# Making the operands of block products kind by kind over the direct tiles, their remainders by adding transfers, and rounding the direct tiles among the block products

## The chip, the core and the metric

The kernel runs on one core of one Trainium2 chip. The core has a matrix engine (TensorE; PE in the profile, with its weight loads as PEld), three elementwise engines (VectorE or DVE, ScalarE or ACT, GpSimd or POOL) and SyncE (SP), whose queue issues most of the loads. Transfers are issued from the queues of SP, ACT or POOL and carried out by 16 DMA engines; a transfer from POOL's queue can add to what stands at its destination. The metric is the time of one execution in microseconds (us); lower is better.

## What is computed

One decoder layer on 512 tokens of width 1024, in float32: two SwiGLU feed-forward halves (inner width 2816) around a hybrid mixer, each behind an RMSNorm, then a last RMSNorm. The change is in the first part of the two feed-forward halves.

```python
def rmsnorm(x, g):
    x32 = x.astype(jnp.float32)
    y = x32 * lax.rsqrt(jnp.mean(x32 * x32, axis=-1, keepdims=True) + EPS)
    return (y * g.astype(jnp.float32)).astype(x.dtype)

def swiglu(x, w_gate, w_up, w_down):
    return (jax.nn.silu(x @ w_gate) * (x @ w_up)) @ w_down
...
x = x + 0.5 * swiglu(rmsnorm(x, ffn1_norm[l]), ffn1_wg[l], ffn1_wu[l], ffn1_wd[l])
x = x + hybrid_mixer(rmsnorm(x, mix_norm[l]), ...)
x = x + 0.5 * swiglu(rmsnorm(x, ffn2_norm[l]), ffn2_wg[l], ffn2_wu[l], ffn2_wd[l])
```

## The kernel before

**Layout.** Features lie on the 128 partitions, the 512 tokens in the columns. The width of 1024 is 8 blocks of 128 (`KD`), the inner width 22 (`KF`). `slot` gives one of 60 buffers of 128x512 floats; a buffer goes back to the pool when the last instruction that touches its tile has run.

**Precision.** Products run in a rounded format, float32r, and each operand is two rounded parts: a rounded copy by ScalarE (`wh` of weights, `yh`, `hh` of activations) and the remainder by VectorE (`wl`, `yl`, `hl`). A product of two operands is three matmuls: high by high, high by low, low by high (`mm3`). `split` (line 260) and `wsplit` (line 238) make such a pair; weights come through `wtiles` with three buffers each for the raw load, the high and the low part.

**A feed-forward half** has an up part (`ffn_up`, line 346) and a down part (`ffn_down`, line 507). In the up part each of 22 inner blocks needs a gate product and an up product over the 8 input blocks.

- *Direct tiles.* The first six blocks of the first half, and the first four of the second, are computed directly: 24 matmuls of 512 columns for the gate, 24 for up. Four of them run in `ffn_up`, before the rest; the first of these four carries the norm's statistics (`norm_steps`), which give `rstd`, the factor of each token. `ffn_act` (line 316) scales both results by `rstd`, applies Silu, multiplies, and splits the result into `hh` and `hl`.
- *Block products.* The other 16 (18 in the second half) are taken in pairs of inner blocks by a scheme of Strassen's kind (`strassen`, line 376): the input is cut into 2 x 2 blocks (four upper input blocks a, four lower b; the token halves `lo` and `hi`), the weights as well, and seven products of half size replace eight. Each of them is 12 matmuls of 256 columns (4 input blocks, 3 matmuls each). Gate and up of a pair follow each other as w = 0, 1, 2, ...; the seven products of one w are interleaved with those of the next. The stream begins, as (product, w): (1,0) (2,0) (6,0) (5,0) (7,0) (1,1) (2,1) (4,0) (6,1) (3,0).
- *Moving operands.* The products use seven kinds of combined input, four columns (j = 0 to 3) of each: `n11` = -a_lo (product 1), `b21` = b_lo (2), `t2` = b_hi - a_hi + a_lo (6), `t1` = a_hi - a_lo (5), `r` = a_hi - b_hi (7), `q` = b_lo - t2 (4), `n22` = -b_hi (3). Each is a tile `cm` of 128x512: the rounded copy in its first 256 columns, the remainder in the last 256. `combine` (line 326) makes all seven kinds of one j after each of the four direct tiles: two scaled copies of x, four subtractions, seven copies by ScalarE and seven remainders by VectorE.
- *Block weights.* `load` (line 392) fetches the raw weights for a w and makes two sums by transfers: SP's queue loads `s1` and `s3`, POOL's queue adds a second load to each (shown as `s`; such an issue is line 161). `prepare` (line 416) runs four products ahead (`LEAD`); for product 6 it adds `s2` = s1 + x on VectorE, and rounds. `results` (line 450) takes finished products out of the accumulators: after product 1 a copy by ScalarE (`tg`), after product 2 a subtraction, and so on; product 6 adds to the accumulator of product 1, so it follows that copy.
- *Rounding of inner blocks.* Results of block products stay float32 (`h`). `halve` (line 500) splits them: four at the end of the stream, the others at the beginning of `ffn_down`.

**What sets the order.** The stream of block products is written out by hand (`manual_schedule`): engines run it in program order. The direct tiles and `combine` before it are ordered when the program is built, by a list scheduler that places instructions on each engine by priority and by its own estimates; each engine then runs its list strictly in order. Every recorded operation has line 173 and every transfer line 161, a helper's; the names of the tiles tell them apart.

Of the kernel before, what the change touches and what calls it, by code (L numbers as in the profile page):

```python
# [9 lines left out]
F32 = mybir.dt.float32  # L10
F32R = mybir.dt.float32r
AF = mybir.ActivationFunctionType
ALU = mybir.AluOpType

P = 128
S = 512
D = 1024
KD = D // P
# [26 lines left out]
HS = S // 2  # L45
LEAD = 4
# [132 lines left out]
def hybrid_kernel(ctx, tc, xt, vec, w1u, w1d, wm, wki, wrg, watt, wrnn, wout, w2u, w2d, out):  # L179
    nc = tc.nc  # L180
    plan = Plan()
    V, A = plan.engine("DVE", nc.vector), plan.engine("ACT", nc.scalar)
    G, T = plan.engine("POOL", nc.gpsimd), plan.engine("PE", nc.tensor)
# [13 lines left out]
    f = lambda ap: ap.bitcast(F32)  # L197
    cnt = [0]
    moving = {}

    def nm(s):
        cnt[0] += 1
        return f"{s}_{cnt[0]}"

    def slot(dt=F32, name="s"):
        return plan.take("slot", big.tile([P, S], dt, tag="slot", name=nm(name)))

    def work(name="t", cols=S):
        return plan.take("tmp", tmp.tile([P, cols], F32, tag="tmp", name=nm(name)))

    def awork(name="a"):
        return patt.tile([P, S], F32, tag="att", name=nm(name))

    def psum(tag="mm"):
        return psp.tile([P, S], F32, tag=tag, name=nm(tag))
# [5 lines left out]
    x = [resid.tile([P, S], F32, name=f"x{k}") for k in range(KD)]  # L221
# [4 lines left out]
    rstd = resid.tile([P, S], F32, name="rstd")  # L226

    def col(base, k):
        return vt[:, base + k:base + k + 1]
# [12 lines left out]
    def wload(src, cols):  # L242
        r, h, l = wtiles(cols)
        Q.dma_start(r, src)
        wsplit(r, h, l)
        return h, l
# [8 lines left out]
    def gemm(ps, w, ys, ks, first=True, last=True, m=P, since=0, upto=None):  # L255
        n = len(ks)
        for i, k in list(enumerate(ks))[since:upto]:
            mm3(ps, w, slice(i * m, (i + 1) * m), ys[k], first and i == 0, last and i == n - 1)

    def split(src, h, l):  # L260
        A.activation(h, src, AF.Copy)
        V.tensor_sub(l, src, f(h))
# [27 lines left out]
    def norm_steps(*sums, blocks=range(NQ)):  # L290
        pc, n = psaux(), len(blocks)
        for i, a in enumerate(sums):
            if i:
                yield waits("PE", a)
            for j, b in enumerate(blocks):

                T.matmul(pc[:, j * QB:(j + 1) * QB], a[:, b * QB:(b + 1) * QB], mean, start=i + j == 0,
                         stop=i == len(sums) - 1 and j == n - 1)
        yield waits("ACT", pc)
        sd = small.tile([P, NQ], F32, tag="st", name=nm("sd"))[:, :n]  # L300
        A.activation(sd, pc.rearrange("p (b c) -> p b c", c=QB)[:, :n, 0], AF.Sqrt, bias=epst)
        yield waits("DVE", sd)
        rs = small.tile([P, NQ], F32, tag="m8", name=nm("rs"))[:, :n]
        V.reciprocal(rs, sd)
        yield waits("PE", rs)
        pb = psaux()[:, :n * QB]
        for j in range(n):
            T.transpose(pb[:, j * QB:(j + 1) * QB], rs[:, j:j + 1].to_broadcast([P, P]), ident)
        yield waits("ACT", pb)
        A.activation(rstd[:, blocks[0] * QB:(blocks[-1] + 1) * QB], pb, AF.Copy)  # L310

    def norm_rest(steps):
        for _ in steps:
            pass

    def ffn_act(pg, pu):
        tg, tu = work("tg"), work("tu")
        V.tensor_mul(tg, pg, rstd)
        A.activation(tg, tg, AF.Silu)
        V.tensor_mul(tu, pu, rstd)  # L320
        V.tensor_mul(tu, tu, tg)
        hh, hl = slot(F32R, "hh"), slot(F32R, "hl")
        split(tu, hh, hl)
        return hh, hl

    def combine(g, j, held):

        lo, hi = slice(0, HS), slice(HS, S)
        a, b, t, q = (slot(F32, n) for n in ("ca", "cb", "ct", "cq"))
        for o, k in ((a, j), (b, j + KD // 2)):  # L330
            V.scalar_tensor_tensor(o, x[k], col(g, k), rstd, op0=ALU.mult, op1=ALU.mult)
        V.tensor_sub(t[:, lo], a[:, hi], a[:, lo])
        V.tensor_sub(t[:, hi], b[:, hi], t[:, lo])
        V.tensor_sub(q[:, lo], b[:, lo], t[:, hi])
        V.tensor_sub(q[:, hi], a[:, hi], b[:, hi])
        for n, src, sign in (("n11", a[:, lo], -1.0), ("b21", b[:, lo], 1.0), ("t2", t[:, hi], 1.0), ("t1", t[:, lo], 1.0),
                             ("r", q[:, hi], 1.0), ("q", q[:, lo], 1.0), ("n22", b[:, hi], -1.0)):
            o = held.pop(0) if len(held) else slot(F32R, "cm")
            if sign > 0:
                split(src, o[:, lo], o[:, hi])  # L340
            else:
                A.activation(o[:, lo], src, AF.Copy, scale=-1.0)
                V.scalar_tensor_tensor(o[:, hi], src, -1.0, f(o[:, lo]), op0=ALU.mult, op1=ALU.subtract)
            moving[n].append(o)

    def ffn_up(y, wu, n0, hs, g, waiting=(), given=()):
        def weights(n, j):
            return given.pop(0) if len(given) else wload(wu[n, j], KD * P)

        moving.update((n, []) for n in ("n11", "b21", "t2", "t1", "r", "q", "n22"))  # L350
        held = []
        for n in range(n0, n0 + 4):
            tag = ("aux", "mm")[n % 2]
            pg, pu = psum(tag), psum(tag)
            gemm(pg, weights(n, 0), y, range(KD))
            w = weights(n, 1)
            if n == n0:
                norm = norm_steps(acc)
                for _ in range(3):
                    next(norm)  # L360
                gemm(pu, w, y, range(KD), last=False, upto=KD // 2)
                norm_rest(norm)
                gemm(pu, w, y, range(KD), first=False, since=KD // 2)
                hs.extend(ffn_act(*p) for p in waiting)
            else:
                gemm(pu, w, y, range(KD))
            hs.append(ffn_act(pg, pu))
            if n == n0:

                for k in ("pth", "ptl"):  # L370
                    t = ptp.tile([P, NQ * S], F32R, tag=k, name=nm("cm"))
                    held.extend(t[:, i * S:(i + 1) * S] for i in range(NQ))
            combine(g, n - n0, held)
        strassen(wu, n0 + 4, hs)

    def strassen(wu, f0, hs):
# [4 lines left out]

        lo, hi = slice(0, HS), slice(HS, S)
        H = KD // 2 * P
        count = KF - f0
        ws, pairs = [], {}
# [4 lines left out]
        def load(w):  # L392

            o = W()
            n, o.j = f0 + w // 2 * 2, w % 2
            o.first = n
            o.x = raw.tile([P, WMAX], F32, tag="raw", name=nm("wr"))
            o.s1, o.s3, o.a22 = (slot(F32, t) for t in ("s1", "s3", "a22"))
            u, v = wu[n, o.j], wu[n + 1, o.j]
            Q.dma_start(o.x, u)  # L400
            Q.dma_start(o.s1, v[:, :H])
            Q.dma_start(o.s3, v[:, :H])
            Q.dma_start(o.a22, v[:, H:])
            G.dma_start(o.s1, v[:, H:], accum_op=ALU.add)
            G.dma_start(o.s3, u[:, :H], accum_op=ALU.add)
            ws.append(o)

        stream = []
# [73 lines left out]
        with tc.manual_schedule(engines=ENGINES):  # L482
            for w in range(2):
                load(w)
            for i in range(LEAD):
                prepare(i)
            for i in range(len(stream)):
                products(i)
                if i:
                    results(i - 1)  # L490
                if i + LEAD < len(stream):
                    prepare(i + LEAD)
                else:
                    n = f0 + i + LEAD - len(stream)
                    halve(hs, n)
                if i % 7 == 3 and len(ws) < count:
                    load(len(ws))
            results(len(stream) - 1)

    def halve(hs, n):  # L500

        if type(hs[n]) is not tuple:
            hh, hl = slot(F32R, "hh"), slot(F32R, "hl")
            split(hs[n], hh, hl)
            hs[n] = hh, hl
# [71 lines left out]
    hs = []  # L577

    class Given:
# [6 lines left out]
        def pop(self, _):  # L586
            return given(self.rs.pop(0))

    ffn_up(y, w1u, 2, hs, V_G1, ((WP[0], WP[1]), (WP[2], pu)), Given(AH[1:]))


# [326 lines left out]
    for k in ("pth", "ptl"):  # L918
        q = ptp.tile([P, NQ * S], F32R, tag=k, name=nm("QI"))
# [319 lines left out]

    hs = []  # L1240
    ffn_up(y2, w2u, 0, hs, V_G2)

    def done(n):
# [11 lines left out]
    n, e = KD - 1, x[KD - 1]  # L1255
# [5 lines left out]
    a, b = CHUNKS[-1]  # L1261
# [33 lines left out]
    o = {}  # L1295
# [75 lines left out]
```

## Time and profile before

| | us |
|---|---|
| median of three runs (lowest, highest) | 1112.08 (1110.92, 1112.80) |
| the profiled execution | 1113.65 |
| its span, first to last instruction | 1111.5 |
| TensorE busy | 1084.1 (98%) |
| VectorE, ScalarE, POOL busy | 773.7, 586.2, 68.7 |
| mean granted clock of TensorE | 0.991 |

A row of the timeline has start, duration, engine, line, operation, out<-in with the names of tiles, and in brackets the idle time of the engine ahead of it with what ended it. Matmuls are pipelined, so their durations overlap, and the distance of two starts is the time that one costs. `PE`, `DVE`, `ACT` and `POOL` are the engines; `SPq` and `POOLq` are their queues. In a row of windows, busy time and count stand for PE, PEld, DVE, ACT and POOL in turn, then the granted clock, the DMA engines' mean share and GB/s. In a row on transfers, "to landing" is the time from an issue to its data standing at the destination.

### The profile page before, as it was taken

To read this page: it belongs to the slowest core of one execution; us is meant where nothing else is said; L and a number is where in the kernel's file an instruction comes from. 1 tells how busy PE (TensorE), PEld (TensorE's weight loads), DVE (VectorE), ACT (ScalarE), POOL (GpSimd) and SP (SyncE) were. 2 spreads that over 40 slices of the span, in tenths; PEclk is the share of its full clock that TensorE was granted. 3 is DMA by queue.
4 is the path that set the end of the run, shared out by engine and by line. 5 is a ranking of instruction groups with operands and counts; after the bars stand their busy time and mean duration, and the time that the engine had idled before them with its cause. 6 is when DMAs were issued, how large, how long until landed. Compare 5 with 4: busy or idle time off the path is not lost.

```text
span 1111.5 us, 16307 instructions
## 1 busy us (share of the span) xinstructions
PE 1084.1 (98%) x6184; PEld 952.2 (86%) x6184; DVE 773.7 (70%) x1412; ACT 586.2 (53%) x1057; POOL 68.7 (6%) x85
## 2 busy tenths in 40 slices
PE   9989999999999989999999999999799999999996
PEld 7869999998888767888888888888699999988885
DVE  6697777786333678998799868557877777783324
ACT  6545555564223458968785664345455555562211
POOL 0011111100000000000000000000011111100001
PEclk9999999999999999999999999999999999999999
DMA  7174777743333352233232213334467777443322
GB/s 267 39 198 116 193 163 185 191 121 87 104 94 92 106 161 63 83 99 98 77 96 79 78 34 99 111 113 139 98 180 163 185 185 196 107 126 104 99 71 75
DMA packets 55949, 135.48 MB, mean 122 GB/s; under 512 B 6592, under 2 KB 11328, under 8 KB 55872
## 3 DMA queue, kind: packets, MB, share of 16 engines
q1 hardware_dynamic: 45936, 116.58, 33.5%
q0 software_dynamic: 9792, 17.83, 10.5%
q8 instruction: 48, 0.79, 0.3%
q14 instruction: 29, 0.24, 0.1%
q10 hardware_dynamic: 144, 0.05, 0.0%
HBM read 130.24 MB, written 2.10 MB: 119 GB/s over the span
## 4 chain that ended last, share of the span: by engine, by line
PE 89%; DVE 6%; ACT 3%; DMA 1%; issue 1%; SPq 0%; DVEq 0%; ACTq 0%
PE mm L173 59%; PE aux L173 30%; DVE wl L173 1%; ACT wh L173 1%; DMA gr<-wrg 1%; DVE yl L173 1%; DVE xc L173 0%; ACT L173 0%; DVE yf L173 0%; DMA x<-xt 0%; DVE o L173 0%; ACT rl L173 0%; DVE tu L173 0%; ACT r L173 0%; DVE th L173 0%
## 5 line engine op out<-in xcount | busy, mean ns | idle before, releaser
L173 DVE TENSOR_TENSOR wl<-wr,wh 128x1024 fp32r<-128x1024 f32 (+3 forms) x204 | 193.0, 954 | 117.2 <-ACT wh L173 113.2
L173 ACT ACTIVATE wh<-wr 128x1024 fp32r<-128x1024 f32 (+4 forms) x206 | 171.2, 836 | 190.5 <-PE mm L173 69.8
L173 PE MATMUL mm<-cm,wh 128*128 128x256 f32 x1088 | 201.5, 285 | 12.0 <-ACT cm L173 6.0
L173 PEld LDWEIGHTS mm<-cm,wh 128*128 128x128 f32 x1088 | 170.9, 193 | 13.7 <-ACT cm L173 6.4
L173 PE MATMUL mm<-yh,wh 128*128 128x512 f32 (+1 forms) x416 | 164.5, 396 | 1.2 <-ACT yh L173 0.7
L173 PE MATMUL mm<-yl,wh 128*128 128x512 f32 (+1 forms) x416 | 162.8, 392 | 0.9 <-DVE yl L173 0.8
L173 PE MATMUL mm<-yh,wl 128*128 128x512 f32 x408 | 159.4, 391 | 0.0
L173 PE MATMUL mm<-cm,wl 128*128 128x256 f32 x544 | 154.7, 284 | 0.0
L173 PE MATMUL aux<-cm,wh 128*128 128x256 f32 x816 | 152.7, 286 | 0.0
L173 ACT ACTIVATE wh<-s 128x512 fp32r<-128x512 f32 x136 | 81.7, 626 | 105.3 <-DVE s L173 72.0
L173 DVE TENSOR_TENSOR wl<-s,wh 128x512 fp32r<-128x512 f32 x136 | 93.5, 690 | 54.0 <-ACT wh L173 50.8
L173 PEld LDWEIGHTS aux<-cm,wh 128*128 128x128 f32 x816 | 129.8, 196 | 0.0
L173 PE MATMUL aux<-cm,wl 128*128 128x256 f32 x408 | 116.8, 286 | 0.0
L173 PEld LDWEIGHTS mm<-cm,wl 128*128 128x128 f32 x544 | 105.2, 193 | 0.0
L173 PEld LDWEIGHTS mm<-yh,wh 128*128 128x128 f32 (+1 forms) x416 | 78.1, 188 | 18.9 <-ACT yh L173 1.9
L173 PEld LDWEIGHTS mm<-yl,wh 128*128 128x128 f32 (+1 forms) x416 | 77.8, 187 | 17.2 <-DVE yl L173 2.1
L173 PEld LDWEIGHTS mm<-yh,wl 128*128 128x128 f32 x408 | 76.7, 188 | 16.3
L173 PEld LDWEIGHTS aux<-cm,wl 128*128 128x128 f32 x408 | 79.7, 195 | 0.0
L173 PE MATMUL mm<-hh,wh 128*128 128x512 f32 (+1 forms) x206 | 78.8, 382 | 0.0
L173 PE MATMUL mm<-hl,wh 128*128 128x512 f32 (+1 forms) x206 | 78.5, 381 | 0.0
L173 PE MATMUL mm<-hh,wl 128*128 128x512 f32 (+1 forms) x206 | 78.5, 381 | 0.0
L173 PE MATMUL aux<-hh,wl 128*128 128x512 f32 x154 | 60.0, 390 | 0.0
(207 smaller groups left out, 1857.1 us busy)
## 6 DMA issues: line engine op xcount, KB each, us to landing
wr<-wm SPq DMA_DIRECT2D x39, 512.0 KB, 3.6
wr<-w2u SPq DMA_DIRECT2D x26, 512.0 KB, 5.0
wr<-w1u SPq DMA_DIRECT2D x21, 512.0 KB, 4.6
s<-w2u SPq DMA_DIRECT2D x36, 256.0 KB, 5.9
s<-w2u POOLq DMA_DIRECT2D x36, 256.0 KB, 4.9
s<-w1u SPq DMA_DIRECT2D x32, 256.0 KB, 4.8
s<-w1u POOLq DMA_DIRECT2D x32, 256.0 KB, 5.3
wr<-w1d SPq DMA_DIRECT2D x16, 448.0 KB, 3.3
```

The costliest lines, as they stand in the source:

```text
L173: return call(*args, **kw)
```

## The change

`ffn_act` ends without the split: it returns the product as one float32 tile from a slot. `halve` now splits these direct tiles within the stream of block products, one after every 14th product, in the order of the blocks.

`combine` has four steps, one after each of the four direct tiles, and each goes over all four j: step 0 makes the scaled copies a and b, `n11` and the difference for r; step 1 makes `b21` and the differences for t1 and t2; step 2 makes `t2`, `t1` and `r`; step 3 makes q's difference, `q` and `n22`. Differences are written in place: t1 over a_hi, t2 over a_lo, q over b_lo. The remainders of `n11` and `n22` stay on VectorE. Those of the other five kinds are made so: ScalarE writes the rounded copy to the first half of `cm` and a second, negated one to its last half, and a transfer from POOL's queue adds the unrounded source to the latter. The eight tiles a and b stay in their slots over all steps; r's difference lies in a buffer of another pool.

```diff
     def ffn_act(pg, pu):
-        tg, tu = work("tg"), work("tu")
+        tg, tu = work("tg"), slot(F32, "h")
...
         V.tensor_mul(tu, tu, tg)
-        hh, hl = slot(F32R, "hh"), slot(F32R, "hl")
-        split(tu, hh, hl)
-        return hh, hl
-
-    def combine(g, j, held):
-        lo, hi = slice(0, HS), slice(HS, S)
-        a, b, t, q = (slot(F32, n) for n in ("ca", "cb", "ct", "cq"))
-        for o, k in ((a, j), (b, j + KD // 2)):
-            V.scalar_tensor_tensor(o, x[k], col(g, k), rstd, op0=ALU.mult, op1=ALU.mult)
-        V.tensor_sub(t[:, lo], a[:, hi], a[:, lo])
-        V.tensor_sub(t[:, hi], b[:, hi], t[:, lo])
-        V.tensor_sub(q[:, lo], b[:, lo], t[:, hi])
-        V.tensor_sub(q[:, hi], a[:, hi], b[:, hi])
-        for n, src, sign in (("n11", a[:, lo], -1.0), ("b21", b[:, lo], 1.0), ("t2", t[:, hi], 1.0), ("t1", t[:, lo], 1.0),
-                             ("r", q[:, hi], 1.0), ("q", q[:, lo], 1.0), ("n22", b[:, hi], -1.0)):
+        return tu
+
+    lo, hi = slice(0, HS), slice(HS, S)
+
+    def combine(g, step, cs, held):
+        def moved(name, src, sign=1.0):
             o = held.pop(0) if len(held) else slot(F32R, "cm")
-            if sign > 0:
-                split(src, o[:, lo], o[:, hi])
+            A.activation(o[:, lo], src, AF.Copy, scale=sign)
+            if sign < 0:
+                V.scalar_tensor_tensor(o[:, hi], src, -1.0, f(o[:, lo]), op0=ALU.mult, op1=ALU.subtract)
             else:
-                A.activation(o[:, lo], src, AF.Copy, scale=-1.0)
-                V.scalar_tensor_tensor(o[:, hi], src, -1.0, f(o[:, lo]), op0=ALU.mult, op1=ALU.subtract)
-            moving[n].append(o)
+                A.activation(o[:, hi], src, AF.Copy, scale=-1.0)
+                G.dma_start(o[:, hi], src, accum_op=ALU.add)
+            moving[name].append(o)
+        for j in range(KD // 2):
+            if step == 0:
+                cs.append((slot(F32, "ca"), slot(F32, "cb"), awork("cr") if j % 2 == 0 else cs[-1][2]))
+            a, b, r = cs[j]
+            r = r[:, (lo, hi)[j % 2]]
+            if step == 0:
+                for o, k in ((a, j), (b, j + KD // 2)):
+                    V.scalar_tensor_tensor(o, x[k], col(g, k), rstd, op0=ALU.mult, op1=ALU.mult)
+                moved("n11", a[:, lo], -1.0)
+                V.tensor_sub(r, a[:, hi], b[:, hi])
+            elif step == 1:
+                moved("b21", b[:, lo])
+                V.tensor_sub(a[:, hi], a[:, hi], a[:, lo])
+                V.tensor_sub(a[:, lo], b[:, hi], a[:, hi])
+            elif step == 2:
+                moved("t2", a[:, lo])
+                moved("t1", a[:, hi])
+                moved("r", r)
+            else:
+                V.tensor_sub(b[:, lo], b[:, lo], a[:, lo])
+                moved("q", b[:, lo])
+                moved("n22", b[:, hi], -1.0)
...
-            combine(g, n - n0, held)
+            combine(g, n - n0, cs, held)
...
                 else:
-                    n = f0 + i + LEAD - len(stream)
-                    halve(hs, n)
+                    halve(hs, f0 + i + LEAD - len(stream))
+                if i % 14 == 12 and i // 14 < f0:
+                    halve(hs, i // 14)
```

More of the change, by code (lines that the diff above doesn't have):

```diff
@@ L350, in ffn_up @@
         moving.update((n, []) for n in ("n11", "b21", "t2", "t1", "r", "q", "n22"))
-        held = []
+        cs, held = [], []
         for n in range(n0, n0 + 4):
@@ L372, in ffn_up @@
                     held.extend(t[:, i * S:(i + 1) * S] for i in range(NQ))
-            combine(g, n - n0, held)
+            combine(g, n - n0, cs, held)
         strassen(wu, n0 + 4, hs)
     def strassen(wu, f0, hs):
-        lo, hi = slice(0, HS), slice(HS, S)
         H = KD // 2 * P
```

## The prediction, made before the changed kernel ran

> **What bounds the kernel now.** I read the page first, then TensorE's groups and timeline, then windows of the clock, then the engines that feed the places where TensorE stands still.
>
> ```profile
> span 1111.5 us, 16307 instructions
> ...
> PE 1084.1 (98%) x6184; PEld 952.2 (86%) x6184; DVE 773.7 (70%) x1412; ACT 586.2 (53%) x1057; POOL 68.7 (6%) x85
> ...
> L173 PE MATMUL mm<-cm,wh 128*128 128x256 f32 x1088 | 201.5, 285 | 12.0 <-ACT cm L173 6.0
> ```
>
> TensorE sets the end nearly everywhere. Its largest wait, 12.0 us of the group that multiplies with the combined operands (cm), lies at two places only: the first block products of each feed-forward half.
>
> ```profile
> 51.88 0.39 PE L173 MATMUL aux<-yh,wh 128*128 128x512 f32 x1
> ...
> 73.64 0.40 PE L173 MATMUL mm<-cm,wh 128*128 128x256 f32 x2
> ...
> 74.59 0.28 PE L173 MATMUL mm<-cm,wl 128*128 128x256 f32 x1
> ...
> 79.89 0.58 PE L173 MATMUL mm<-cm,wh 128*128 128x256 f32 x1 [1.63 <-DVE cm L173]
> ...
> 84.54 0.80 PE L173 MATMUL mm<-cm,wh 128*128 128x256 f32 x2 [1.29 <-ACT tg L173]
> ...
> 89.38 0.40 PE L173 MATMUL mm<-cm,wh 128*128 128x256 f32 x2
> ...
> 767.20 0.39 PE L173 MATMUL aux<-yh,wh 128*128 128x512 f32 x1
> ...
> 788.96 0.40 PE L173 MATMUL mm<-cm,wh 128*128 128x256 f32 x2
> ...
> 789.91 0.28 PE L173 MATMUL mm<-cm,wl 128*128 128x256 f32 x1
> ...
> 799.88 0.51 PE L173 MATMUL mm<-cm,wh 128*128 128x256 f32 x2 [1.42 <-ACT tg L173]
> ...
> 802.86 0.40 PE L173 MATMUL mm<-cm,wh 128*128 128x256 f32 x2
> ```
>
> These are starts. 51.88 and 767.20 begin the third direct tile of each half; 96 matmuls later, at (73.64 - 51.88) / 96 = 0.2267 us each, block products begin. A block product is 12 matmuls at 0.12 us, 1.44 us. 84.54 and 799.88 are the third product, 89.38 and 802.86 the fifth. Four products should take 5.76 us; they take 15.74 and 13.90, so the two transitions lose 9.98 + 8.14 = 18.1 us. That is all the change could win.
>
> ```profile
> 75.00:78.50 3.50, 0.38 (x1) 0.19 (x1) 2.80 (x6) 1.46 (x3) 1.64 (x2) 1.00 1.06 262
> 78.50:88.50 10.00, 7.32 (x32) 7.02 (x33) 7.42 (x18) 5.53 (x13) 0.11 (x1) 0.50 0.40 69
> ...
> 89.40:235.00 145.60, 145.60 (x1216) 145.60 (x1215) 106.80 (x193) 79.29 (x167) 22.79 (x26) 1.00 0.69 168
> ...
> 795.50:798.50 3.00, 2.97 (x14) 2.67 (x13) 2.27 (x6) 1.15 (x4) 0.00 (x0) 0.50 0.00 0
> ```
>
> The columns are busy PE, PEld, DVE, ACT and POOL, granted clock, DMA share, GB/s. Part of the loss is clock: it fell to 0.50 after TensorE had emptied, and stayed there some 10 us in the first transition and 3 in the second. Behind the transition TensorE is busy without a gap.
>
> **Step 1: the direct tiles.** Per half, VectorE loses 20 remainders (kinds b21, t2, t1, r, q) and the splits of the direct tiles; ScalarE gains 20 negated copies; POOL's queue gains 20 adding transfers. What the saving buys depends on the order in the built program. There VectorE makes all four columns of one kind before it goes on, and the weight remainder wl for the third direct tile's gate now stands behind two such steps. TensorE's order has moved with it: two matmuls of that gate, two of its up part, two of the next gate, and then it waits for that wl. Durations on VectorE, by the distance of starts:
>
> ```profile
> 39.08 0.69 DVE L173 TENSOR_TENSOR tg<-mm,rstd 128x512 f32<-128x512 f32 x1 [2.08 <-ACT rstd L173]
> ...
> 47.42 0.75 DVE L173 SCALAR_TENSOR_TENSOR ca<-x,vt,rstd 128x512 f32<-128x512 f32 x1
> 48.08 0.75 DVE L173 SCALAR_TENSOR_TENSOR cb<-x,vt,rstd 128x512 f32<-128x512 f32 x1
> 48.74 0.42 DVE L173 TENSOR_TENSOR ct<-ca 128x256 f32<-128x256 f32 x1
> 49.08 0.42 DVE L173 TENSOR_TENSOR cq<-ca,cb 128x256 f32<-128x256 f32 x1
> ...
> 52.43 0.69 DVE L173 TENSOR_TENSOR tg<-mm,rstd 128x512 f32<-128x512 f32 x1
> 53.03 0.69 DVE L173 TENSOR_TENSOR tu<-mm,rstd 128x512 f32<-128x512 f32 x1
> 53.63 1.22 DVE L173 TENSOR_TENSOR wl<-wr,wh 128x1024 fp32r<-128x1024 f32 x1
> ...
> 81.77 0.68 DVE L173 TENSOR_TENSOR s<-s,wr 128x512 f32<-128x512 f32 x1
> ...
> 756.51 0.69 DVE L173 TENSOR_TENSOR tu<-aux,rstd 128x512 f32<-128x512 f32 x1 [1.43 <-PE aux L173]
> ```
>
> 0.60 us for a 512-column product, 0.66 for a scaled one, 0.34 for 256 columns, 1.22 for a weight remainder to its end. First half: from 39.08, where the order is still the old one, 12 x 0.60 + 8 x 0.66 + 15 x 0.34 = 17.6 us stand ahead of that wl; it ends at 39.08 + 17.6 + 1.22 = 57.9. TensorE runs dry at 51.88 + 6 x 0.2267 = 53.24: a new gap of 4.6 us. Second half, from 756.51: 5 x 0.60 + 8 x 0.66 + 15 x 0.34 = 13.4, so 771.1 against 768.56: 2.5 us. The other operands that TensorE needs there are in time. The sum over both is 7.2 us, and block products begin at 78.3 and 791.5.
>
> **Step 2: the transition.** No combined operand holds it up any more: n11 and b21 are done one and two tiles earlier, q and n22 are needed only by the eighth and tenth product. The first two products take 2.88 us, to 81.2 and 794.4. The third needs the weight sum s2, and with it s1, the sum that an adding transfer of POOL makes. In POOL's order s1's transfer now stands behind 16 adding transfers of t2, t1, r and q; and its copy of the first product (tg) stands on ScalarE behind the three rounded copies of s2, s1, s3, as before.
>
> ```profile
> 49.80 0.40 ACT L173 ACTIVATE cm<-cq 128x256 fp32r<-128x256 f32 x1
> 50.11 0.40 ACT L173 ACTIVATE cm<-ct 128x256 fp32r<-128x256 f32 x1
> ...
> 51.85 1.06 ACT L173 ACTIVATE wh<-wr 128x1024 fp32r<-128x1024 f32 x1 [0.89 <-PE mm L173]
> ...
> 82.55 1.67 ACT L173 ACTIVATE wh<-s 128x512 fp32r<-128x512 f32 x3 [1.82 <-DVE s L173]
> 84.12 0.36 ACT L173 ACTIVATE tg<-mm 128x256 f32<-128x256 f32 x1
> ```
>
> ```profile
> L161 POOL DMA_DIRECT2D s<-w2u x36: 862/865/1242, 771.7 to 954.9; - x36
> L161 POOL DMA_DIRECT2D s<-w1u x32: 856/870/1147, 63.0 to 220.8; - x32
> ...
> DMA to landing us min/median/max: 3.8/5.2/7.9
> ```
>
> The 24 copies of t2, t1 and r stand on ScalarE behind the first rounded block weights, whose buffer is free when TensorE has made the 43rd matmul after the gap: 57.9 + 43 x 0.2267 + 0.15 = 67.8 (0.15: what a matmul's end lies behind the next start). With 0.52 for those weights (a third of 84.12 - 82.55) and two copies of 0.31, POOL's first of them issues at 69.0. ScalarE makes a pair in 0.61 us, POOL issues in 0.87, so POOL sets the pace: 16 x 0.87 = 13.9, s1 issues at 82.9. Landing 5.2 gives 88.1. From s2's start to the third product took 84.54 - 81.77 = 2.77 us: 90.9 against 84.54, 6.4 us later. Second half: 771.1 + 9.75 + 0.15 + 0.52 + 0.7 = 782.2, + 13.9 + 5.2 + 2.77 = 804.1 against 799.88, 4.2 later.
>
> TensorE stands still from 81.2 to 90.9 and from 794.4 to 804.1, longer than before, so the clock falls again. The old rows had 3 to 10 us at half clock; nothing stalls behind the third product now, so I stay near the shorter row: 4.2 us, losing 2.1 (bounds 1.5 and 2.9, when both products run at half). Third and fourth product then take 2.88 + 2.1 = 5.0, against 89.38 - 84.54 = 4.84 and 802.86 - 799.88 = 2.98. Fifth product: 95.9 against 89.38, +6.5; 809.1 against 802.86, +6.2.
>
> Neither an adding transfer of 128x256 nor one from SBUF is in the trace. POOL's issue: if it goes by rows of descriptors, 0.87; if by bytes, 0.44. I take 0.87, since 128 partitions stay. At 0.44 ScalarE sets the pace (last q copy at 80.2), s1 issues 2.2 us earlier in each half. Landing: 3.8 to 7.9, I take the median. Whether the engines keep up:
>
> ```profile
> q0 software_dynamic: 9792, 17.83, 10.5%
> ...
> q0 software_dynamic: 218, 0.39, 113.0%
> ```
>
> The second row is of 78 to 80 us, when only adding transfers ran: 0.39 MB in 2 us. By bytes 0.131 MB takes 0.67 us, less than 0.87, and nothing queues. By packets (9792 / 68 = 144 a transfer) it takes 2 x 144 / 218 = 1.32, and 16 of them 7.2 us longer than POOL's issues. I take bytes, since a packet is half as long here.
>
> The Trainium skill (DMA: Bandwidth & Descriptors, Anatomy of one DMA — SWDGE (gpsimd) path) gives a transfer of POOL about 2.0 us plus its bytes at 436 GB/s. For 256 KB that is an estimate of 2.6 us. The shortest landing in the trace is 3.8, so the measurement decides; by the page the sum would be 2 x 2.6 less.
>
> **Step 3: rounding the direct tiles among the products.** Ten more pairs, 0.62 on ScalarE and 0.69 on VectorE each, one in 14 products. They lie beside TensorE: in the window of 145.60 us VectorE has 38.8 idle, ScalarE 66. I cost them at nothing; without that cover, 10 x 1.3 = 13 us. Their sources keep one slot instead of two, and the down products' order is unchanged. The four in-place subtractions for q wait for the landings of b21's adds. The last of these issues behind the two copies after the weights rounded from 51.85, near 54, and lands near 59.5; the subtractions stand two weight remainders behind the 57.9 of step 1, near 60.4.
>
> **Sum.** +6.5 + 6.2 = +12.7 us. The profiled execution took 1113.65 (span 1111.5 and 2.15 around it), the median of the three is 1112.08: 1126.4 for the one, 1125 for the other.
>
> **Rivals.**
> - Cheap adds (0.44, or a landing near 3.8). For it: half the bytes. Against it: as many rows; the trace has one size of adding transfer only. 12.7 - 2 x 2.2 = +8.3, 1120; with both +5.5, 1117.6.
> - Adds queue in the engines. For it: 113% at 218 packets. Against it: the shorter packet. 12.7 + 2 x 7.2 = +27, 1139.
> - The clock falls in the 4.6 us gap too. It fell between 3.6 and 5.3 us after TensorE emptied (74.87 to 78.5; 790.2 to 795.5), so it may. Some 2 us, 1127. The Trainium skill (TensorE: Matmul & The Clock Gate, Part 1: The HAM clock gate) speaks of a free-running idle window of 3.4 us; by it a 4.6 us gap would hold a whole one in about a third of executions, and the rows agree.
> - Faster: s1's transfer lands before the second product ends. At its place, POOL's queue, that needs an issue by 81.2 - 2.77 - 5.2 = 73.2 in the first half, 4.2 us after the first add could go; a product then follows at once, and only step 1's 7.2 us stays of the 18.1: 1101. Against it: ScalarE alone finishes q at 80.2.
> - That TensorE's wait moves and nothing is won or lost needs s1 some 5 us earlier in both halves.
>
> **How the numbers follow.** Forecast of 1121 to 1131 (with the clock's fall): 0.52. Cheap adds, 1114.5 to 1121: 0.22. Queueing, 1131 to 1141: 0.16; beyond 0.02. Faster 0.05. Within 0.2%, about what a measurement of this kernel can tell from no change: 0.03. So faster 0.05, same 0.03, slower 0.92. The range 1116 to 1138 takes in the cheap end with both bounds and the queueing end.
>
> **What would show it.** TensorE idle some 4.6 us near 53 and 2.5 near 769, released by VectorE's wl; 16 issues of cm on POOL in a row at 0.87 ahead of s; the third product near 91 and 804, released by ScalarE's tg; no wait for cm. If the group on cm shows no new gap in the direct tiles, step 1 is wrong; if s1 issues before 75, step 2 is.

## The result and the profile after

| | us |
|---|---|
| changed kernel, median of four runs (lowest, highest) | 1139.88 (1138.63, 1142.12) |
| kernel before on the same chip, median of four | 1112.44 (1110.92, 1113.04) |
| ratio, with its 95% interval | 1.0251 (1.0231 to 1.0271) |
| the profiled execution after, its span | 1140.51, 1138.7 |

The change costs 27.4 us, 2.5%. The sign was forecast; the size was not: 1125 was expected, and 1139.88 lies above the range of 1116 to 1138. The page of the kernel after:

```profile
span 1138.7 us, 16398 instructions
...
PE 1092.4 (96%) x6184; PEld 956.1 (84%) x6184; DVE 760.7 (67%) x1372; ACT 597.0 (52%) x1097; POOL 104.3 (9%) x125
...
L173 PE MATMUL mm<-cm,wh 128*128 128x256 f32 x1088 | 202.6, 286 | 22.8 <-ACT tg L173 22.8
```

VectorE is busy 13 us less, as the change has it, and the wait for `cm` is gone. The same group now waits nearly twice as long, 22.8 us against 12.0, and all of it for `tg`. The same starts as before, in TensorE's timeline of the kernel after:

```profile
52.68 0.39 PE L173 MATMUL aux<-yh,wh 128*128 128x512 f32 x1
...
58.82 0.80 PE L173 MATMUL aux<-yh,wl 128*128 128x512 f32 x1 [4.27 <-DVE wl L173]
...
82.27 0.40 PE L173 MATMUL mm<-cm,wh 128*128 128x256 f32 x2
...
94.89 0.80 PE L173 MATMUL mm<-cm,wh 128*128 128x256 f32 x2 [9.59 <-ACT tg L173]
...
99.72 0.40 PE L173 MATMUL mm<-cm,wh 128*128 128x256 f32 x2
...
780.89 0.39 PE L173 MATMUL aux<-yh,wh 128*128 128x512 f32 x1
...
782.30 0.50 PE L173 MATMUL mm<-yh,wh 128*128 128x512 f32 x1 [0.34 <-ACT wh L173]
...
784.82 0.50 PE L173 MATMUL aux<-yh,wl 128*128 128x512 f32 x1 [1.79 <-DVE wl L173]
...
806.98 0.40 PE L173 MATMUL mm<-cm,wh 128*128 128x256 f32 x2
...
820.92 0.80 PE L173 MATMUL mm<-cm,wh 128*128 128x256 f32 x2 [10.90 <-ACT tg L173]
...
826.21 0.40 PE L173 MATMUL mm<-cm,wh 128*128 128x256 f32 x2
...
842.43 0.51 PE L173 MATMUL mm<-cm,wh 128*128 128x256 f32 x2 [0.23 <-ACT tg L173]
...
904.35 0.50 PE L173 MATMUL mm<-cm,wh 128*128 128x256 f32 x2 [0.23 <-ACT tg L173]
```

The two gaps for `wl` and the two long waits of the third product are where the prediction put them. The last two rows belong to something that it had at nothing: behind the transitions the stream of block products, without a gap before, now has a short wait once in each 14 products. From 842.43 to 904.35 there are three such cycles of (904.35 - 842.43) / 3 = 20.64 us; 14 products at 1.44 are 20.16. So each of the ten rounded direct tiles costs 0.48 us.

The tile `hh`, the rounded inner blocks, marks where the down products begin and end. First the kernel before, then the kernel after (minimum, median and longest duration in ns, then the first and the last start):

```profile
L173 PE MATMUL mm<-hh,wh x206: 283/389/416, 244.9 to 1100.4; 128*128 128x512 f32 x95, 128*128 128x256 f32 x8
```

```profile
L173 PE MATMUL mm<-hh,wh x206: 278/389/408, 258.1 to 1125.4; 128*128 128x512 f32 x95, 128*128 128x256 f32 x8
```

At the first down product the kernel after is 13.2 us late, at the last 25.0. Set against the prediction's stages, each a distance of starts after less the same before:

| stage | predicted, both halves | measured, first + second half |
|---|---|---|
| up to the third direct tile | 0 | 0.80 |
| third direct tile to first block product | 4.6 + 2.5 = 7.1 | 7.83 + 4.33 = 12.2 |
| first to fifth block product | 1.9 + 3.7 = 5.6 | 1.71 + 5.33 = 7.0 |
| the other block products | 0 | 6 x 0.48 + 4 x 0.48 = 4.8 |
| between the halves, and the down part behind | 0 | 0.45 - 0.25 = 0.2 |
| behind the last down product | 0 | 27.2 - 25.0 = 2.2 |
| sum | 12.7 | 27.2 (span 1138.7 - 1111.5) |

The first and the fifth row, 1.0 us together, are of the size by which executions of one kernel differ (1138.63 to 1142.12): the first run below, whose edit lies behind that point, begins its third direct tile at 51.76, not at 52.68. The last row is not scatter. From the last down product of these rows to the end of the span pass 11.1 us before and 13.3 after. In the runs below it is 11.1 to 11.4 in the three without adding transfers of combined operands, 12.0 in the one with 24 of them, and 13.3 to 13.6 in the six with all 40. The last output transfer lands 0.9 us ahead of the end before and 3.1 after; what grew is a wait behind it, when the engines meet at the kernel's close. SyncE's waits there, before and after (total, times, longest):

```profile
SPq L1367 <- PEq L1367: 0.7, 2, 0.5
```

```profile
SPq L1385 <- PEq L1385: 2.9, 2, 2.4
```

So these 2.2 us go with the adding transfers; why is not shown. The second, third and fourth row are what the experiments are about. The second is more than its gaps. Windows of the kernel after (columns as before, the granted clock third from the end):

```profile
54.50:58.80 4.30, 0.05 (x1) 0.00 (x0) 4.25 (x11) 0.39 (x1) 0.87 (x1) 0.93 0.21 30
58.80:64.00 5.20, 5.18 (x12) 4.12 (x13) 3.91 (x7) 0.00 (x0) 0.00 (x0) 0.50 0.64 171
64.00:66.00 2.00, 2.00 (x8) 1.53 (x8) 0.00 (x0) 0.00 (x0) 0.00 (x0) 0.74 1.02 390
...
785.50:786.50 1.00, 1.00 (x4) 0.81 (x3) 1.00 (x2) 0.00 (x0) 0.00 (x0) 0.50 0.92 90
```

The clock fell at the end of the gap, and the busy TensorE worked at half of it until about 65. From 58.82 on, 90 matmuls stand ahead of the first block product; at 0.2267 us they take 20.4, and they took 82.27 - 58.82 = 23.45, so the clock cost 3.05 beside the 4.78 of the gap itself (58.82 - 52.68, less six matmuls). In the second half the same sum gives 784.82 - 780.89 - 1.36 = 2.57 for the gap and 806.98 - 784.82 - 20.4 = 1.76 for the clock.

### The profile page after: what moved, and what is told of

Same layout as the page of the kernel before. It is cut to its first block, busy times and chain, and to the rows that moved or that the text cites. A ratio compares the mean times of both kernels' runs of the same rounds, so it can differ in the third digit from the quotient of the medians.

```text
span 1138.7 us, 16398 instructions
## 1 busy us (share of the span) xinstructions
PE 1092.4 (96%) x6184; PEld 956.1 (84%) x6184; DVE 760.7 (67%) x1372; ACT 597.0 (52%) x1097; POOL 104.3 (9%) x125
## 3 DMA queue, kind: packets, MB, share of 16 engines
q0 software_dynamic: 15552, 23.08, 13.3%
## 4 chain that ended last, share of the span: by engine, by line
PE 79%; DVE 7%; ACT 5%; DMA 5%; issue 2%; POOL 1%; SPq 1%; DVEq 0%; ACTq 0%; POOLq 0%
PE mm L173 54%; PE aux L173 25%; ACT wh L173 2%; DVE wl L173 2%; DMA a<-w1u 2%; DVE s L173 1%; POOL cm L161 1%; ACT cm L173 1%; DMA s<-w2u 1%; DMA gr<-wrg 1%; DMA s<-w1u 1%; ACT hh L173 1%; DVE yl L173 1%; SPq L161 1%; DMA x<-xt 0%
## 5 line engine op out<-in xcount | busy, mean ns | idle before, releaser
L173 PE MATMUL mm<-cm,wh 128*128 128x256 f32 x1088 | 202.6, 286 | 22.8 <-ACT tg L173 22.8
```

The lines of the kernel that those rows point to most:

```text
L173: return call(*args, **kw)
```

## The experiments

Times are medians; each ratio is to the kernel before, measured on the same chip in the same hours. A saving against the change compares two series; the kernel before took 1111.9 to 1112.9 us in them.

### The rounding at another place

```diff
-                if i % 14 == 12 and i // 14 < f0:
-                    halve(hs, i // 14)
+                if i % 14 == 3 and 0 < i // 14 <= f0:
+                    halve(hs, i // 14 - 1)
```

> The rounding of a direct tile among the products moves by five products in the cycle of fourteen, behind the first copy of the block weights a22, where ScalarE stands idle some 2.9 us. Theory (a rounding copy that stands ahead of a product's copy on ScalarE holds the product's buffer, 0.47 us in each of ten cycles): ten of the twelve waits for tg go, 1139.9 - 4.7 = 1135.2 us. Rival (the rounding costs nothing, as step 3 had it, and the short waits belong to the products' own rhythm): 1139.9, twelve waits as before.

1133.96 us, ratio 1.0196 (1.0178 to 1.0214): 5.9 us less than the change, where the theory had 4.7. First the wait of TensorE in the kernel after, then in this run (total, times, longest):

```profile
PE mm L173 <- ACT tg L173: 22.8, 12, 10.9
```

```profile
PE mm L173 <- ACT tg L173: 20.2, 2, 10.7
```

All ten short waits are gone. What made them stands in ScalarE's timeline of the kernel after, in one of those cycles:

```profile
861.60 0.63 ACT L173 ACTIVATE wh<-s 128x512 fp32r<-128x512 f32 x1 [1.94 <-DVE s L173]
862.14 0.61 ACT L173 ACTIVATE hh<-h 128x512 fp32r<-128x512 f32 x1
862.66 0.36 ACT L173 ACTIVATE tg<-mm 128x256 f32<-128x256 f32 x1
...
865.61 0.62 ACT L173 ACTIVATE wh<-a 128x512 fp32r<-128x512 f32 x1
```

The `hh` copy stands right ahead of the `tg` copy that takes a product out of its accumulator, and TensorE's product 6 adds to that accumulator. It makes that copy 0.52 us later, and TensorE loses 0.48 by its starts; the trace counts only 0.23 of them as idle, since matmuls overlap in it (one of 256 columns lasts 0.28 and costs 0.12). Behind the last row ScalarE is idle until 869.12; there the same copy costs nothing.

### The next weights ahead of the combining step

```diff
-            gemm(pg, weights(n, 0), y, range(KD))
-            w = weights(n, 1)
+            gemm(pg, ready.pop(0) if ready else weights(n, 0), y, range(KD))
+            w = ready.pop(0) if ready else weights(n, 1)
...
+            if n < n0 + 3:
+                ready.extend(weights(n + 1, j) for j in range(2))
             combine(g, n - n0, cs, held)
```

> The weights of the next direct tile are loaded and split ahead of the combining step. Theory (the late wl cost its gap and, through the clock, as much again; what follows is tied to TensorE's progress): the direct tiles lose 7.8 and 4.3 us of excess, 1139.9 - 12.1 = 1128, and the third products come as much earlier. Rival 1 (only the gaps count, the clock falls anyway): 1139.9 - 6.1 = 1134. Rival 2 (POOL's adding transfers set the third product whatever TensorE does before): the time comes back there, 1138 to 1140.

1129.03 us, ratio 1.0146 (1.0131 to 1.0161): 10.9 less than the change, near the theory's 12.1. TensorE's timeline of this run:

```profile
52.44 0.39 PE L173 MATMUL aux<-yh,wh 128*128 128x512 f32 x1
...
55.50 0.50 PE L173 MATMUL aux<-yh,wl 128*128 128x512 f32 x1 [1.19 <-DVE wl L173]
...
76.03 0.40 PE L173 MATMUL mm<-cm,wh 128*128 128x256 f32 x2
...
89.11 0.80 PE L173 MATMUL mm<-cm,wh 128*128 128x256 f32 x2 [10.05 <-ACT tg L173]
```

A gap of 1.19 is left in the first half and none in the second. Behind it the 90 matmuls take 76.03 - 55.50 = 20.53 us, the full pace: with the long gap the fall of the clock is gone too. The gaps shrank by 4.27 + 1.79 + 0.34 - 1.19 = 5.2, the time by twice that. The third product's wait moved along with TensorE (10.05 against 9.59), so rival 2 falls: the chain through POOL begins at TensorE's progress and doesn't run beside it.

### The first weight sums ahead of the combined operands

```diff
+            if n == n0 + 1:
+                early = [sums(wu, n0 + 4, w) for w in range(2)]
             combine(g, n - n0, cs, held)
...
+        G.dma_start(s1, v[:, H:], accum_op=ALU.add)
+        G.dma_start(s3, u[:, :H], accum_op=ALU.add)
...
-            G.dma_start(o.s1, v[:, H:], accum_op=ALU.add)
-            G.dma_start(o.s3, u[:, :H], accum_op=ALU.add)
+            o.s1, o.s3 = early.pop(0) if early else sums(wu, f0, w)
```

> The first four adding transfers of weight sums (s1 and s3 of two parts) are issued ahead of the sixteen of combined operands. Theory (the queue on POOL in front of s1 is all that holds the third product): the first four products take 6 us instead of 17.5 and 19.4, 1139.9 - 24.8 = 1115. Rival (the transfer engines are the limit, so what goes first only changes which operand is late): TensorE waits for cm instead, 1125 to 1139.

1121.39 us, ratio 1.0078 (1.0063 to 1.0093): 18.5 less than the change, of the theory's 24.8. TensorE's timeline in the first half, and then VectorE's:

```profile
79.70 0.40 PE L173 MATMUL mm<-cm,wh 128*128 128x256 f32 x2
...
85.37 0.80 PE L173 MATMUL mm<-cm,wh 128*128 128x256 f32 x2 [2.64 <-ACT tg L173]
...
89.59 0.40 PE L173 MATMUL mm<-cm,wh 128*128 128x256 f32 x2
```

```profile
81.24 1.43 DVE L173 SCALAR_TENSOR_TENSOR cm<-cb,cm 128x256 fp32r<-128x256 f32 x4
82.58 0.68 DVE L173 TENSOR_TENSOR s<-s,wr 128x512 f32<-128x512 f32 x1
```

The third product waits 2.64 us instead of 9.59, for no `cm`: the sixteen transfers were all that kept s1 from it, and their own data are needed late enough. The rest has another owner. `s2` (82.58) stands on VectorE behind four remainders of `n22`, and the copies of s2, s1 and s3 stand on ScalarE ahead of `tg`.

### Half of the adding transfers

```diff
-                moved("r", r)
+                moved("r", r, add=False)
...
-                moved("q", b[:, lo])
+                moved("q", b[:, lo], add=False)
```

With `add=False` the remainder is a subtraction on VectorE.

> The change with the remainders of r and q on VectorE: eight adding transfers instead of sixteen stand ahead of s1 on POOL. Theory (the third product follows the number of transfers in that queue): s1 issues some 5 us earlier in each half and lands sooner, since the transfer engines are less full, so 10 to 14 us less than 1139.9, 1126 to 1130. Rival (ScalarE's copies or the engines' time set the pace): under 4 us less, 1136 or more.

1126.02 us, ratio 1.0121 (1.0106 to 1.0137): 13.9 less than the change, the far end of the theory. The wait for `tg` fell from 22.8 to 10.0, at most 3.8 at once, and VectorE no longer waits for the transfer of s1, which it did for 6.9 and 7.6 us in the kernel after. Eight transfers fewer are enough to take POOL off the path; what is left is `s2` on VectorE behind the remainders of q and n22. Eight copies of ScalarE go with the transfers, so this run alone can't tell the two apart; the run before it, which keeps every copy, does.

### All remainders on VectorE

```diff
-                A.activation(o[:, hi], src, AF.Copy, scale=-1.0)
-                G.dma_start(o[:, hi], src, accum_op=ALU.add)
+                V.tensor_sub(o[:, hi], src, f(o[:, lo]))
```

> Combining by kind as in the change, but all remainders on VectorE and no adding transfer of combined operands. Theory (the order by kind costs the gaps in the direct tiles, the transfers cost the wait of the third product): the gaps grow by four remainders, 1.4 us in each half, the third product's wait goes, 1139.9 - 24.8 + 2.8 = 1118. Rival (VectorE can't make the remainders in time, which is what the kernel before shows): a wait for cm comes back, 1125 or more.

1127.28 us, ratio 1.0131 (1.0114 to 1.0148): 12.6 less than the change: the rival's range, not the theory's 1118. TensorE's waits in this run:

```profile
PE mm L173 <- ACT tg L173: 10.0, 12, 3.9
PE aux L173 <- DVE wl L173: 8.9, 2, 5.5
```

The gaps grew as expected (4.27 to 5.50 in the first half). No wait for `cm` came back, so the rival's reason is wrong all the same; the third product still waits 3.85 us in each half, since VectorE now makes `s2` behind remainders of `q` and `n22`. Combining by kind without any adding transfer still loses 14.6 us to the kernel before: gaps, clock and rounding need no transfer for it.

### Rounding among the products alone, in the kernel before

```diff
-        tg, tu = work("tg"), work("tu")
+        tg, tu = work("tg"), slot(F32, "h")
...
-        hh, hl = slot(F32R, "hh"), slot(F32R, "hl")
-        split(tu, hh, hl)
-        return hh, hl
+        return tu
...
+                if i % 14 == 12 and i // 14 < f0:
+                    halve(hs, i // 14)
```

> The kernel before with nothing but step 3 of the change: direct tiles are kept whole and rounded among the block products, at the change's own places. Theory (each of the ten roundings holds TensorE 0.47 us, and the last direct tile's rounding, 1.35 us on the chain ahead of the combined operands, is taken out of the transition of each half): 1112 + 4.7 - 2.7 = 1114 us, ten short waits for tg. Rival (step 3 as predicted, covered): no short waits, 1109 to 1112.

1115.92 us, ratio 1.0030 (1.0020 to 1.0040). The waits of TensorE in this run:

```profile
PE mm L173 <- ACT tg L173: 7.8, 12, 2.7
PE mm L173 <- DVE cm L173: 4.5, 2, 2.2
```

Ten waits more than the two of the kernel before, and the time is 3.0 above it: ten times 0.48, less what the transitions gained (2.1 us by the starts). Step 3 taken alone makes the kernel slower too.

### The three repairs together, and further

The first run has the three edits above in one kernel (rounding later, weights first, sums first).

> The three edits in one kernel: rounding five products later, weights of the next direct tile ahead of the combining step, first weight sums ahead of the combined operands. Theory (three separate causes, whose costs add): 1139.9 - 5.9 - 10.9 - 18.5 = 1104.6 us, below the kernel before. Rival (one and the same chain, the second edit uncovers what the first hid): 1112 to 1120.

1107.37 us, ratio 0.9957 (0.9942 to 0.9972): the edits save 32.5 us together, where the three alone saved 5.9 + 10.9 + 18.5 = 35.3. So the causes are separate and nearly additive, and with the three repairs the change is 0.4% faster than the kernel before.

```diff
+            if n == n0 + 3:
+                x0, s2 = raw.tile([P, WMAX], F32, tag="raw", name=nm("wr")), slot(F32, "s2")
+                Q.dma_start(x0, wu[n0 + 4, 0])
+                V.tensor_add(s2, early[0][0], x0[:, :KD // 2 * P])
             combine(g, n - n0, cs, held)
```

> As the run with the three edits, and the sum s2 is made by VectorE ahead of the four remainders of n22. Theory (the third product's remaining 2.6 us stand on VectorE's order, four remainders of 0.34 ahead of s2): 1.3 us less in each half and as much again by the clock, 1104.6 - 2.6 to 5.2 = 1099.4 to 1102. Rival (ScalarE's copy of the first product is late by its own queue, not by s2): no change, 1104.6.

1101.48 us, ratio 0.9902 (0.9885 to 0.9918), the fastest of all, 1% below the kernel before. TensorE's timeline of this run in the first half:

```profile
75.78 0.40 PE L173 MATMUL mm<-cm,wh 128*128 128x256 f32 x2
...
80.00 0.51 PE L173 MATMUL mm<-cm,wh 128*128 128x256 f32 x2 [1.18 <-ACT tg L173]
...
82.98 0.40 PE L173 MATMUL mm<-cm,wh 128*128 128x256 f32 x2
```

Four products in 7.20 us, against 17.45 in the change, 15.74 before and 5.76 without any wait. The clock didn't fall: the third product's row lasts 0.51 (0.80 in the runs quoted above), and third and fourth product take 82.98 - 80.00 = 2.98 us. The run with the three edits had kept its clock in the first half as well; in the second its third and fourth product took 4.48 us, against 3.07 here. By the starts the two transitions gain 4.8 of the 5.9 us; the rest is not accounted for.

With all remainders on VectorE in place of the adding transfers, on the kernel with the three edits:

> As the run with the three edits, with all remainders on VectorE and no adding transfer of combined operands. Theory (with the sums first the adding transfers stand in nobody's way, and VectorE has idle time enough in the last two direct tiles): as with the transfers, 1104.6 within 2 us. Rival (VectorE is what the adding transfers relieve): 1108 or more, with a wait of TensorE for VectorE's cm or wl.

1109.56 us, ratio 0.9975 (0.9966 to 0.9984), 2.2 above the same kernel with the transfers. The number is the rival's, and the adding transfers do relieve VectorE, but the loss isn't a wait for VectorE's `cm` or a larger one for `wl` (still 1.2). It is again the third product behind `s2`, 3.8 us in place of 2.6. With that the first four products take 23.5 us over both halves instead of 18.8; 2.4 of these 4.7 us come back at the kernel's close, where no adding transfer of operands lengthens the wait.

At last, `n22` made in the third step instead of the fourth, on top of the fastest:

> As the run with s2 ahead, and n22 is made in the third step instead of the fourth, which takes its copies and remainders from ScalarE and VectorE ahead of the first products. Theory: the third product's wait goes, 5.3 us and the clock's share with it, 1104.6 - 5.3 to 10 = 1095 to 1099. Rival (the copy of the first product then waits for something later, such as the s1 or s3 of the sums or a buffer of wh): 1100 to 1105.

1101.95 us, ratio 0.9907 (0.9892 to 0.9922): no gain, the rival's number. ScalarE's timeline of this run shows what holds `tg`:

```profile
75.33 2.55 ACT L173 ACTIVATE cm<-cb 128x256 fp32r<-128x256 f32 x8
77.79 1.66 ACT L173 ACTIVATE wh<-s 128x512 fp32r<-128x512 f32 x3
79.35 0.36 ACT L173 ACTIVATE tg<-mm 128x256 f32<-128x256 f32 x1
```

The copies of s2, s1 and s3 follow those of q without a pause, in this run as in the fastest. So ScalarE's own list is the limit now, and `n22` made earlier only moves its four copies ahead in the same list: `tg` comes 3.8 us behind the first product's start in both.

## Why the prediction was wrong

**Step 1, the gaps: right in place, cause and size; its price incomplete.** Predicted 4.6 and 2.5 us, found 4.78 and 2.57. The prediction then made the rest of the direct tile run at full pace and put the fall of the clock into a rival, at "some 2 us". It fell in both gaps, for 3.05 + 1.76 = 4.8 us; the run with the weights ahead shows gap and fall going together. The prediction priced exactly such a fall two paragraphs later, in the transition, from rows of the kernel before in which the clock fell 3.6 to 5.3 us after TensorE had emptied. The Trainium skill (TensorE: Matmul & The Clock Gate, Part 1: The HAM clock gate) asks for a whole idle window of some 3.4 us. The gap of 4.27 agrees. The second half's 1.79, with two matmuls ahead of it and a gap of 0.34 before those, had the clock at 0.50 as well (785.50 to 786.50); here the measurement decides, and a gap well under 3.4 us was enough. Nor does the length alone decide: in the first half a wait of 2.64 us brought the clock down in the run with the sums first (0.80 for the row behind it), and one of 2.63 didn't in the run with the three repairs.

**Step 2, the transition: right in mechanism, near in size.** The third product came behind 16 transfers, released by `tg`, as forecast. From the first of them to s1's landing 13.9 + 5.2 = 19.1 us were predicted, and 18.66 passed (73.40 to 92.06). POOL's timeline of the kernel after:

```profile
73.40 1.75 POOL L161 DMA_DIRECT2D cm<-ca  x2 [17.86 <-DVE wl L173]
74.63 1.41 POOL L161 DMA_DIRECT2D cm<-cr  x1
...
80.16 3.88 POOL L161 DMA_DIRECT2D cm<-cr  x1
81.82 5.78 POOL L161 DMA_DIRECT2D cm<-cb  x4
85.14 3.35 POOL L161 DMA_DIRECT2D s<-w1u  x1
```

The starts follow ScalarE's pairs of copies (0.61 us apart for t2, t1 and r), but the rows overlap and grow, so a start isn't yet POOL's work on that transfer. Its pace is the distance of the ends: the third transfer ends at 76.04, the sixteenth at 87.60, which is 11.56 / 13 = 0.89 us each, and s1's own at 88.49. So POOL did set the pace, near the predicted 0.87. A transfer of 128x256 that stands alone, of b21 near 50, takes 0.85 to 0.87 as well, so the choice of 0.87 over 0.44 was right. s1 lands 3.6 us behind its row's end, where 5.2 - 0.87 = 4.3 were forecast.

In the first half the four products took 17.45 against 17.6 predicted. In the second they took 19.23. Its rows in the timelines of VectorE and ScalarE:

```profile
817.50 0.69 DVE L173 TENSOR_TENSOR s<-s,wr 128x512 f32<-128x512 f32 x1 [7.56 <-DMA s<-w2u]
...
819.96 0.63 ACT L173 ACTIVATE wh<-s 128x512 fp32r<-128x512 f32 x1 [0.51 <-DMA s<-w2u]
```

There s1 landed 817.5 - 798.11 = 19.4 us behind the start of the first transfer, 0.3 more than forecast. From s2 to the third product 820.92 - 817.50 = 3.42 passed instead of 2.77, since ScalarE's last copy ahead of `tg` waited for a second adding transfer, of s3. The two products behind lost 2.4 us to the clock (826.21 - 820.92 = 5.29), not 2.1. And the first transfer went out 8.9 us ahead of the first block product, not 791.5 - 782.2 = 9.3. Together that is 1.6 of the miss. The runs with the sums ahead and with half the transfers show that the number of transfers ahead of s1 is the cause.

**Step 3, the rounding: the step that failed outright.** It was costed at nothing because ScalarE has 66 us and VectorE 38.8 idle in a window of 145.60. That is a mean. At the place where the change puts it, the copy stands in a strict order right ahead of the copy that frees TensorE's accumulator, and it costs 0.48 us each time, 4.8 in all. Both runs that move it or try it alone show this.

**The rivals.** The queue in the transfer engines forecast 1139, which is what was measured, for another reason: it wanted 7.2 us more in each transition, and the transitions missed by -0.2 and +1.6. The cheap adds, the early s1 and no net change fell. The clock's fall was right for the first gap, 3.05 us against some 2, and left out the second, 1.76.

So of the 14.5 us between 12.7 and 27.2, 4.8 are the clock behind the gaps, 4.8 the rounding, 2.2 the wait at the kernel's close, 1.4 the transitions, 0.8 + 0.2 scatter, and 0.25 the gaps. The first two are terms that the sum had at nothing, and experiments show both; the third no step had, and its cause is open.

## What to carry to other kernels

Idle time of an engine that runs its list in order is no cover by itself: look at which instruction the new one stands in front of, and who waits for that one. Price a new gap of TensorE by its length and by the half clock behind it, which here cost 4.8 us beside 7.4 of gaps. Work that is taken from a busy engine and given to a queue is paid by what stands behind it in that queue; put what is needed first ahead of it. With that, with the weights and `s2` ahead of the combining steps and the rounding at another place, this change turned from 2.5% slower to 1% faster.

## What was not expected of the hardware

The queue of adding transfers in the kernel after, from 77 to 81 us (packets, MB, share of the 16 engines' time):

```profile
q0 software_dynamic: 615, 0.56, 100.1%
```

By these shares the engines were full with 0.14 MB/us in adding transfers alone. 4 x 16 x 1.001 / 615 is 0.104 us a packet, where the kernel before took 2 x 16 x 1.13 / 218 = 0.166 us for packets of about twice the size: half the bytes cost 0.63 of the time, between the prediction's two readings (by bytes, by packets). At 144 packets a transfer takes 0.94 us of all engines, about POOL's pace of 0.89.

Yet no transfer of combined operands waits long in the engines. The third of the sixteen lands 3.6 us after its row's start and the twelfth 6.3, but their rows on POOL last 1.41 and 3.88 (above), so they land 2.2 and 2.4 us behind their ends. What grows along the queue is the time in POOL, and a share of 100% was no sign of a queue in the engines.
